# Sliding-window caches loaded once for all four groups, unchanged cache rows copied HBM to HBM, first group's sample rows two tiles later

## The chip, the core and the metric

The kernel runs on one core of one Trainium2 chip. The metric is the device time of one execution in microseconds, as the median of several runs; lower is better.

## What is computed

One inference step of a hybrid decoder layer, in float32, for 1024 prompt tokens and 8 sample tokens (one new token for each of 8 requests). From the normalised tokens `h` one wide projection gives the inputs of two branches, retention (4 heads) and sliding-window attention (16 query heads in 4 groups, one key and value head of 64 for each group); both are gated, projected, merged by sigmoid gates and projected once more. The change concerns the sample tokens of the sliding-window branch:

```python
def swa_sample(q, k, v, sinks, cache_k, cache_v):
    kk = jnp.concatenate([cache_k.astype(k.dtype), k], axis=1)
    vv = jnp.concatenate([cache_v.astype(v.dtype), v], axis=1)
    ...
    o = sink_attention(q[:, None], kk[:, None], vv[:, None], allowed, sinks)[:, 0]
    return o, kk[:, Ts:], vv[:, Ts:]
```

The caches are (8 requests, 128 rows, 4 groups, 64). Each request attends to the last 127 cached rows and its new row. The outputs `ks` and `vs` are the caches moved up by one row, with the new row at the end: 127 of 128 rows of each are copies of the input.

## The kernel before

All matrix products run on TensorE as three products of a split into an upper and a lower half (`hi`, `lo`). A weight unit is loaded into `wraw` on SP's queue (`load_unit`, L162), ACT makes the upper half `whi` (L168), and POOL the lower half `wlo` (L169). There are three `wraw` buffers and six of each half, and `run_steps` loads units ahead of their use.

`groups` builds one long list of steps: first the loading and normalising of the tokens (`norm_h`), then eight groups, four of retention (`ret_tile`, `ret_rows`) and four of sliding window (`swa_tile`, `swa_rows`). A group goes over eight tiles of 128 tokens. In each tile a product of 128 tokens with 384 columns (`gemm_tok`, L222 to L224) is followed by the tile's other stages, which are spread over the next tiles as a pipeline, and between them stand fill blocks: gates of the group before (`gate_block`, products L212 to L214, then tanh on ACT, a product on DVE and, on POOL, L288) and merge gates (`mg_block`, whose results leave on ACT's own DMA queue, L299). `FILL`, `TAIL` and `ROW` say how many fill blocks a group gets, how many come after its last tile, and after which tile the 8 sample rows of a group start. The rows run as stages as well, one after each following tile.

`swa_rows` of a group g takes these steps: load the 127 last rows of the group's keys into `cK` and of its values into `cV` (L569, L570; partition = cache row, so a DMA writes 127 partitions of 8 rows of 64 floats, 256 B each); project the 8 sample rows (`gemm_rows`, L232, L233, and L237 into `rkv`), rope and norm (`kd`); put the new key and value into partition 127 (L575, L576); store the whole of `cK` and `cV` to the outputs (L577, L578); then, one stage each, transpose queries (L585) and keys (L592), scores (L599), softmax, product with the values (L612). `cK` and `cV` have one buffer each.

`swa_consts` runs once, when the sliding-window groups begin: it loads rope tables, band, sinks (L848, eight small DMAs).

The order on each engine and queue is not the order of the code: a scheduler puts the instructions of all steps in an order by its own times, and each engine then takes them strictly in that order. An instruction that waits holds all that stand behind it on its engine. Every DMA of SP goes to one queue that is served by up to 16 DMA engines; a DMA of SP also waits for the DMA eight places ahead of it that used its semaphore.

Of the kernel before, what the change touches and what calls it, by code (L numbers as in the profile page):

```python
# [17 lines left out]
P = 128  # L18
D = 1024
SEQ = 1024  # L20
NS = 8
# [6 lines left out]
SH, KVH, G, HD = 16, 4, 4, 64  # L28
# [25 lines left out]
QAT = (1, 2, 4)  # L54
ROW = [2, 0, 0, 0, 0, 0, 0, 1]
FILL = [3, 2, 2, 2, 9, 9, 9, 4]
# [66 lines left out]
class Body:  # L123
# [25 lines left out]

# [1 line left out]
    def load_unit(self, spec):  # L151
# [46 lines left out]

# [1 line left out]
    def mm3(self, ps, a, b, start=True, stop=True):  # L200
# [37 lines left out]

# [1 line left out]
    def norm_h(self, t):  # L240
# [36 lines left out]

# [1 line left out]
    def gate_block(self, unit, kt, nb, oT, i):  # L279
# [20 lines left out]

# [1 line left out]
    def ret_q(self, unit, qT, nb):  # L302
# [145 lines left out]

# [1 line left out]
    def rope_s(self, dst, src, A, B, nh, t, p=P):  # L450
# [114 lines left out]
    def swa_rows(self, g, units, oT):  # L565
        nc = self.nc
        K = self.t(self.ap, [P, NS, HD], "cK", bufs=1)
        V = self.t(self.ap, [P, NS, HD], "cV", bufs=1)
        nc.sync.dma_start(out=K[: P - 1], in_=self.i["cache_swa_k"][0, :, 1:, g, :].rearrange("b k d -> k b d"))  # L569
        nc.sync.dma_start(out=V[: P - 1], in_=self.i["cache_swa_v"][0, :, 1:, g, :].rearrange("b k d -> k b d"))  # L570
        acc = self.t(self.pacc, [P, 512], "acc")
        kv = self.t(self.ap, [NS, 384], "rkv", bufs=1)
        self.gemm_rows(acc[:MROW, :384], units, self.hs, kv[:], 384)
        qr, kd, rs = self.swa_rope(kv[:], NT, NS)
        nc.sync.dma_start(out=K[P - 1 : P], in_=kd[:NS, 0, :])  # L575
        nc.sync.dma_start(out=V[P - 1 : P], in_=kv[:, 320:384])  # L576
        nc.sync.dma_start(out=self.o["ks"][0, :, :, g, :].rearrange("b k d -> k b d"), in_=K[:])  # L577
        nc.sync.dma_start(out=self.o["vs"][0, :, :, g, :].rearrange("b k d -> k b d"), in_=V[:])  # L578
        qn = self.t(self.ap, [NS, G, 2, HD], "rbig", bufs=1)
# [9 lines left out]
        pt = self.t(self.ptr, [P, 512], "tr")  # L589
        kc = K[:].rearrange("p b d -> p (b d)")  # L590
        for i in range(NS // 2):
# [4 lines left out]
        R = NS * G  # L596
# [11 lines left out]
        pTs = self.t(self.ap, [P, R], "pTs", bufs=1)  # L608
        nc.scalar.activation(out=pTs[:], in_=pt[:, :R], func=AF.Copy)
        yield  # L610
        po = self.t(self.pav, [P, 512], "av")
        nc.tensor.matmul(po[:R], pTs[:], V[:].rearrange("p b d -> p (b d)"), start=True, stop=True)  # L612
        od = self.t(self.ap, [R, NS, HD], "rbig", bufs=1)
# [32 lines left out]

# [1 line left out]
    def build(self):  # L648
# [38 lines left out]
    def groups(self):  # L687
        nc = self.nc
# [16 lines left out]
        def gates(gi, st):  # L705
            for i in range(2):
                kt = 2 * gi + i
                col = (OFF_RG + kt * P) if gi < 4 else (OFF_SG + (kt - 8) * P)
                for nb in range(NB):
                    yield ([tch(col)], (lambda us, kt=kt, nb=nb, i=i: self.gate_block(us[0], kt, nb, st["o"], i)))  # L710
# [10 lines left out]
        kv = slabs([(OFF_RK, DK), (OFF_RV, DV)])  # L721
# [12 lines left out]
        def rope_block(nb):  # L734
# [3 lines left out]
            return ([], fn, 0)  # L738

        def tables(us):  # L740
            nc.sync.dma_start(out=self.ropeK[:], in_=self.i["c_ropeK"][:])
            nc.sync.dma_start(out=self.misc[:], in_=self.i["c_misc"][:])
            nc.sync.dma_start(out=self.maskT[:], in_=self.i["c_maskT"][:])
# [12 lines left out]
        for gi in range(8):  # L756
# [5 lines left out]
            if ret:  # L762
# [10 lines left out]
                kv = slabs([(OFF_RK + h * DK, DK), (OFF_RV + h * DV, DV)])  # L773
                mk = lambda u, t, h=h, st=st: self.ret_tile(h, t, u, st["q"], st, st["o"])
                mkr = lambda u, h=h, st=st: self.ret_rows(h, u, st["q"], st["o"])
            else:
                g = gi - 4
# [7 lines left out]
                kv = slabs([(OFF_SQ + g * G * HD, G * HD), (OFF_SK + g * HD, HD), (OFF_SV + g * HD, HD)])  # L785
# [30 lines left out]
            if extra:  # L816
                pipe = []
            prev = list(gates(gi, st))

# [15 lines left out]
    def swa_consts(self):  # L835
        nc, ap = self.nc, self.ap
        self.swa_tables()
        nc.sync.dma_start(out=self.rng[:], in_=self.i["ret_norm_g"][0].rearrange("h (i p) -> p (h i)", p=P))
        nc.vector.tensor_scalar(out=self.rng[:], in0=self.rng[:], scalar1=0.5, scalar2=None, op0=ALU.mult)
        self.band = self.t(ap, [P, 2 * P], "band")  # L840
        nc.sync.dma_start(out=self.band[:], in_=self.i["c_band"][:])
        self.sink = self.t(ap, [P, SH], "sink")
        nc.sync.dma_start(out=self.sink[:], in_=self.i["swa_sinks"][0:1, :].broadcast_to([P, SH]))
        self.nsink = self.t(ap, [P, SH], "nsink")
        nc.vector.tensor_scalar(out=self.nsink[:], in0=self.sink[:], scalar1=-1.0, scalar2=None, op0=ALU.mult)
        self.sinkr = self.t(ap, [NS * G, KVH], "sinkr")
        for b in range(NS):
            nc.sync.dma_start(out=self.sinkr[b * G : (b + 1) * G, :], in_=self.i["swa_sinks"][0].rearrange("(g j) -> j g", g=KVH))  # L848
        self.nsinkr = self.t(ap, [NS * G, KVH], "nsinkr")
        nc.vector.tensor_scalar(out=self.nsinkr[:], in0=self.sinkr[:], scalar1=-1.0, scalar2=None, op0=ALU.mult)  # L850

    def split_op(self, pool, tag, src, kt):
# [121 lines left out]
```

## Time and profile before

| | |
|---|---|
| time, median of 3 runs | 1224.25 us (1223.89 to 1225.06) |
| span of the profiled execution | 1217.8 us |
| between that span and the median | 6.45 us |
| TensorE busy | 1178.2 us, 97% of the span |
| VectorE, ScalarE, GpSimd busy | 679.5, 457.9, 353.5 us |
| mean granted TensorE clock | 0.993 of full speed |
| moved by DMA | 116.69 MB, mean 96 GB/s |
| largest wait of TensorE | 17.7 us |

The page gives, for one execution, the busy time of each engine, the span in 40 slices of 30.4 us with the busy share in tenths, and the groups of instructions that cost most. The trace can be asked for more: who waited for whom, the instructions of one engine in order of time, and for any stretch the busy time, the granted clock (1.00 is 2.4 GHz, 0.50 is 1.2 GHz), the busy share of the 16 DMA engines (transfers that overlap on an engine count twice, so it can pass 1) and the GB/s. SPq stands for SP's DMA queue, and the time of a row there is the time that issuing took, not the transfer.

### The profile page before, as it was taken

Reading aid. Unit: us, or ns where it says so; the run is one execution under the profiler, and the core shown is the slowest. Engines: PE = TensorE matmul, PEld = TensorE weight load, DVE = VectorE, ACT = ScalarE, POOL = GpSimd, SP = SyncE. Lnnn points to the kernel's source line nnn. Section 1 sums busy time; section 2 is a strip of 40 time slices with the busy share of each in tenths; the row PEclk is TensorE's granted clock in tenths of the full one; section 3 lists DMA queues with packets and bytes.
Section 4 is the critical chain, followed back from the end, with each engine's and each line's share of the span. In section 5 each row is a group of like instructions: output and inputs, shape, how many; then the busy total and the mean of one; then the engine's idle time right before and its main releaser. Section 6 shows DMA issues by size and latency. Waiting matters only on the chain.

```text
span 1217.8 us, 19525 instructions
## 1 busy us (share of the span) xinstructions
PE 1178.2 (97%) x7228; PEld 1112.4 (91%) x7228; DVE 679.5 (56%) x2018; ACT 457.9 (38%) x1158; POOL 353.5 (29%) x278
## 2 busy tenths in 40 slices
PE   5999999999999859999999999999999999999998
PEld 5899999999999759999999999999899999999876
DVE  5854554544554438787677688578854411565121
ACT  6544342443343124554454445444544310221010
POOL 5434035116126312331342125222523122122010
PEclk9999999999999979999999999999999999999999
DMA  9133204214114112230142014201516844554221
GB/s 321 49 94 102 68 22 123 75 42 122 59 37 121 58 32 63 79 105 20 36 132 82 16 36 125 72 24 36 170 41 230 249 143 144 170 162 136 79 88 69
DMA packets 139368, 116.69 MB, mean 96 GB/s; under 512 B 33760, under 2 KB 127456, under 8 KB 139272
## 3 DMA queue, kind: packets, MB, share of 16 engines
q1 hardware_dynamic: 132360, 106.98, 29.0%
q10 hardware_dynamic: 6912, 8.46, 2.0%
q8 instruction: 57, 0.93, 0.3%
q14 instruction: 39, 0.32, 0.1%
HBM read 82.95 MB, written 32.44 MB: 95 GB/s over the span
## 4 chain that ended last, share of the span: by engine, by line
PE 89%; DVE 4%; DMA 2%; SPq 1%; ACT 1%; issue 1%; POOL 1%; ACTq 0%; POOLq 0%
PE acc L212 15%; PE acc L213 15%; PE acc L214 15%; PE acc L224 9%; PE acc L223 9%; PE acc L222 9%; PE tr L546 2%; DVE s L491 1%; DMA cV<-rkv 1%; PE acc L233 1%; PE acc L232 1%; PE av L441 1%; PE sc L532 1%; PE sc L533 1%; SPq L570 1%; PE av L557 1%
## 5 line engine op out<-in xcount | busy, mean ns | idle before, releaser
L169 POOL TENSOR_TENSOR wlo<-wraw,whi 128x1024 fp32r<-128x1024 f32 (+1 forms) x92 | 205.2, 2240 | 333.7 <-ACT whi L168 276.4
L212 PE MATMUL acc<-hhi,whi 128*128 128x344 f32 x864 | 281.2, 326 | 0.6 <-ACT tg L298 0.6
L213 PE MATMUL acc<-hlo,whi 128*128 128x344 f32 x864 | 278.4, 322 | 0.0
L214 PE MATMUL acc<-hhi,wlo 128*128 128x344 f32 x864 | 278.3, 323 | 0.0
L222 PE MATMUL acc<-whi,hhi 128*128 128x384 f32 x512 | 174.7, 342 | 1.7 <-ACT hhi L139 1.3
L224 PE MATMUL acc<-whi,hlo 128*128 128x384 f32 x512 | 174.9, 342 | 0.0
L223 PE MATMUL acc<-wlo,hhi 128*128 128x384 f32 x512 | 174.3, 340 | 0.6 <-POOL wlo L169 0.6
L212 PEld LDWEIGHTS acc<-hhi,whi 128*128 128x128 f32 x864 | 163.1, 189 | 2.8 <-ACT tg L298 0.9
L213 PEld LDWEIGHTS acc<-hlo,whi 128*128 128x128 f32 x864 | 162.9, 188 | 1.9 <-issue 1.0
L214 PEld LDWEIGHTS acc<-hhi,wlo 128*128 128x128 f32 x864 | 162.7, 188 | 1.1 <-issue 0.4
L147 POOL TENSOR_TENSOR rs<-ms,nhalf 128x1 f32<-128x1 f32 (+3 forms) x81 | 69.4, 859 | 322.4 <-DVE ms L146 318.1
L168 ACT ACTIVATE whi<-wraw 128x1024 fp32r<-128x1024 f32 (+1 forms) x92 | 90.1, 982 | 156.2 <-PE acc L213 97.9
L222 PEld LDWEIGHTS acc<-whi,hhi 128*128 128x128 f32 x512 | 96.6, 189 | 3.1 <-ACT hhi L139 1.7
L223 PEld LDWEIGHTS acc<-wlo,hhi 128*128 128x128 f32 x512 | 96.6, 189 | 2.4 <-POOL wlo L169 1.0
L224 PEld LDWEIGHTS acc<-whi,hlo 128*128 128x128 f32 x512 | 96.5, 188 | 0.8 <-DVE hlo L140 0.2
L486 ACT ACTIVATE s<-s,ng 128x256 f32<-128x256 f32 (+1 forms) x128 | 61.7, 485 | 27.0 <-DVE ng L483 26.6
L288 POOL TENSOR_TENSOR oT<-oT,tg 128x344 f32<-128x344 f32 x48 | 45.7, 954 | 88.3 <-DVE tg L286 60.7
L536 DVE CUSTOM_DVE_ANT_0 s<-sc,band,rs 128x256 f32<-128x256 f32 (+1 forms) x128 | 53.6, 459 | 13.1 <-PE sc L533 12.8
L139 ACT ACTIVATE pThi<-tr 128x512 fp32r<-128x512 f32 x60 | 35.3, 597 | 52.3 <-PE tr L546 51.8
L140 DVE TENSOR_TENSOR pTlo<-tr,pThi 128x512 fp32r<-128x512 f32 x60 | 40.9, 685 | 23.0 <-ACT pThi L139 22.6
L491 DVE TENSOR_SCALAR s<-s,r 128x256 f32<-128x256 f32 (+1 forms) x128 | 52.9, 475 | 0.7
L224 PE MATMUL acc<-whi,mlo 128*128 128x512 f32 x128 | 50.5, 395 | 0.0
(345 smaller groups left out, 2365.1 us busy)
## 6 DMA issues: line engine op xcount, KB each, us to landing
wraw<-in_w_in SPq DMA_DIRECT2D x36, 512.0 KB
d_t<-tg ACTq DMA_DIRECT2D x48, 172.0 KB
d_o<-oT SPq DMA_DIRECT2D x16, 516.0 KB
tt<-d_t SPq DMA_DIRECT2D x48, 172.0 KB
wraw<-in_w_in SPq DMA_DIRECT2D x32, 256.0 KB
st<-d_o SPq DMA_DIRECT2D x9, 516.0 KB
d_m<-tt SPq DMA_DIRECT2D x24, 172.0 KB
mm<-d_m SPq DMA_DIRECT2D x24, 172.0 KB
```

Of the source, the lines that this page charges most:

```text
L147: nc.gpsimd.tensor_tensor(out=rs[:p, :width], in0=ms[:p, :width], in1=self.nhalf[:p, :width], op=ALU.pow)
L168: nc.scalar.activation(out=hi[:, :f], in_=raw[:, :f], func=AF.Copy)
L169: nc.gpsimd.tensor_tensor(out=lo[:, :f], in0=raw[:, :f], in1=hi[:, :f].bitcast(F32), op=ALU.subtract)
L212: nc.tensor.matmul(ps, whi[:, k, :], hi[:, cs], start=(k == 0), stop=False)
L213: nc.tensor.matmul(ps, whi[:, k, :], lo[:, cs], start=False, stop=False)
L214: nc.tensor.matmul(ps, wlo[:, k, :], hi[:, cs], start=False, stop=(k == KT - 1))
L222: nc.tensor.matmul(ps, hi[:, k, a:b], whi[:, kk, :], start=(k == 0), stop=False)
L223: nc.tensor.matmul(ps, hi[:, k, a:b], wlo[:, kk, :], start=False, stop=False)
L224: nc.tensor.matmul(ps, lo[:, k, a:b], whi[:, kk, :], start=False, stop=(k == KT - 1))
L486: nc.scalar.activation(out=s[:p, j, :nk], in_=s[:p, j, :nk], func=AF.Exp, bias=ng[:p, j : j + 1], accum_out=l[:p, j : j + 1])
L491: nc.vector.tensor_scalar(out=s[:p, j, :nk], in0=s[:p, j, :nk], scalar1=r[:p, j : j + 1], scalar2=None, op0=ALU.mult)
L536: nc.vector.tensor_tensor_reduce(out=s[:, j, :nk], in0=sc[:, a, :nk], in1=band, scale=rs[:, j : j + 1], scalar=-3e38, op0=ALU.add, op1=ALU ...
```

## The change

The loads of `cK` and `cV` leave `swa_rows`. Two tiles of (128, 8, 256) are kept for all four groups, and `swa_consts` loads each of them once, in rows of 1 KB (all four groups of one cache row of one request). `swa_rows` works on the 64 columns of its group, and POOL first copies the group's keys into a dense tile `kc` for the transposes. Only the new row is stored from SBUF; the 127 unchanged rows are copied from the input to the output in HBM, by `shift`, a step put behind group 1's tiles. Group 4 of the list (the first sliding-window group) has its rows two tiles later (`ROW`).

```diff
-ROW = [2, 0, 0, 0, 0, 0, 0, 1]
+ROW = [2, 0, 0, 0, 2, 0, 0, 1]
...
     def swa_rows(self, g, units, oT):
         nc = self.nc
-        K = self.t(self.ap, [P, NS, HD], "cK", bufs=1)
-        V = self.t(self.ap, [P, NS, HD], "cV", bufs=1)
-        nc.sync.dma_start(out=K[: P - 1], in_=self.i["cache_swa_k"][0, :, 1:, g, :].rearrange("b k d -> k b d"))
-        nc.sync.dma_start(out=V[: P - 1], in_=self.i["cache_swa_v"][0, :, 1:, g, :].rearrange("b k d -> k b d"))
+        gs = slice(g * HD, (g + 1) * HD)
+        K, V = self.cK[:, :, gs], self.cV[:, :, gs]
...
         nc.sync.dma_start(out=K[P - 1 : P], in_=kd[:NS, 0, :])
         nc.sync.dma_start(out=V[P - 1 : P], in_=kv[:, 320:384])
-        nc.sync.dma_start(out=self.o["ks"][0, :, :, g, :].rearrange("b k d -> k b d"), in_=K[:])
-        nc.sync.dma_start(out=self.o["vs"][0, :, :, g, :].rearrange("b k d -> k b d"), in_=V[:])
+        nc.sync.dma_start(out=self.o["ks"][0, :, P - 1, g, :], in_=kd[:NS, 0, :])
+        nc.sync.dma_start(out=self.o["vs"][0, :, P - 1, g, :], in_=kv[:, 320:384])
...
-        kc = K[:].rearrange("p b d -> p (b d)")
+        kc = self.t(self.ap, [P, NS, HD], "kc", bufs=1)
+        nc.gpsimd.tensor_copy(out=kc[:], in_=K)
+        kc = kc[:].rearrange("p b d -> p (b d)")
...
-        nc.tensor.matmul(po[:R], pTs[:], V[:].rearrange("p b d -> p (b d)"), start=True, stop=True)
+        nc.tensor.matmul(po[:R], pTs[:], V, start=True, stop=True)
...
+        def shift(us):
+            for o, name in (("ks", "cache_swa_k"), ("vs", "cache_swa_v")):
+                nc.sync.dma_start(
+                    out=self.o[o][0, :, : P - 1].rearrange("b k g d -> b (k g d)"),
+                    in_=self.i[name][0, :, 1:].rearrange("b k g d -> b (k g d)"),
+                )
...
+            if gi == 1:
+                put(([], shift))
...
     def swa_consts(self):
         nc, ap = self.nc, self.ap
+        self.cK = self.t(ap, [P, NS, KVH * HD], "cK")
+        self.cV = self.t(ap, [P, NS, KVH * HD], "cV")
...
+        for dst, name in ((self.cK, "cache_swa_k"), (self.cV, "cache_swa_v")):
+            nc.sync.dma_start(out=dst[: P - 1], in_=self.i[name][0, :, 1:].rearrange("b k g d -> k b (g d)"))
...
-    nc = bacc.Bacc("TRN2", target_bir_lowering=False, num_devices=1)
+    nc = bacc.Bacc("TRN2", target_bir_lowering=False, num_devices=1, dynamic_dma_scratch_size=1024)
```

The scheduler moves more than the diff tells. First, SP's queue near the start of the program, as a difference of the two orders (the line numbers are those of each kernel; `ropeT`, `rng` and `oT` are tables, norm weights and tiles of x, `wraw_270` holds the query weights of the first group):

```order
 L737 DMA ropeT_140<-in_c_ropeT 128x2x344
-L838 DMA rng_111<-in_ret_norm_g 128x8x1
+L742 DMA out_ks<-in_cache_swa_k 8x2x16256
+L742 DMA out_vs<-in_cache_swa_v 8x2x16256
 L162 DMA wraw_270<-in_w_in 128x8x128
+L849 DMA rng_111<-in_ret_norm_g 128x8x1
 L251 DMA oT_299<-in_x_prompt 128x1024 x2
 L162 DMA wraw_398<-in_w_in 128x8x128
```

The copies of `shift`, written behind group 1, stand ahead of the query weights and of the last tiles of x; the load of `rng` has gone behind those weights.

Second, SP's queue where the sliding-window groups begin, before and then after (`sinkr` are the small tables, `wraw_6055` the first weights of the second sliding-window group):

```order
L848 DMA sinkr_4809<-in_swa_sinks 4x4x1 x8
L569 DMA cK_4899<-in_cache_swa_k 127x8x64
L570 DMA cV_4900<-in_cache_swa_v 127x8x64
L576 DMA cV_4900<-rkv_4904 1x8x64
L578 DMA out_vs<-cV_4900 128x8x64
L575 DMA cK_4899<-kd_4944 1x8x64
L577 DMA out_ks<-cK_4899 128x8x64
L569 DMA cK_6359<-in_cache_swa_k 127x8x64
L162 DMA wraw_6055<-in_w_in 128x2x256
```

```order
L859 DMA sinkr_4813<-in_swa_sinks 4x4x1 x8
L863 DMA cK_4780<-in_cache_swa_k 127x8x256
L863 DMA cV_4781<-in_cache_swa_v 127x8x256
L574 DMA cV_4781<-rkv_5137 1x8x64
L576 DMA out_vs<-rkv_5137 8x64
L573 DMA cK_4780<-kd_5177 1x8x64
L575 DMA out_ks<-kd_5177 8x64
L162 DMA wraw_6055<-in_w_in 128x2x256
```

The two loads keep their place and their 127 partitions, and their rows grow from 64 to 256 floats; the new rows still follow them on the queue.

Third, POOL in the first sliding-window group, before and then after (`oT<-oT,tg` is a gate's product, `rs` a tile's rstd, `wlo_5341` before and `wlo_5309` after the lower half of the next gate block's weights):

```order
L147 TENSOR_TENSOR rs_5180<-ms_5179,nhalf_68 128x5
L288 TENSOR_TENSOR oT_3572<-oT_3572,tg_5298 128x344
L169 TENSOR_TENSOR wlo_5341<-wraw_5339,whi_5340 128x1024
L288 TENSOR_TENSOR oT_3572<-oT_3572,tg_5334 128x344
L147 TENSOR_TENSOR rs_5375<-ms_5374,nhalf_68 128x5
```

```order
L288 TENSOR_TENSOR oT_3574<-oT_3574,tg_5266 128x344
L589 COPY kc_5371<-cK_4780 128x512
L169 TENSOR_TENSOR wlo_5309<-wraw_5307,whi_5308 128x1024
L288 TENSOR_TENSOR oT_3574<-oT_3574,tg_5302 128x344
L147 TENSOR_TENSOR rs_5343<-ms_5342,nhalf_68 128x5
```

The copy of the keys stands directly ahead of that lower half. On PE the same gate block now has this beginning, behind the last products of a tile, and the transposes of the keys come only after it:

```order
L224 MATMUL acc_5313<-whi_4836,hlo_122 128x384
L212 MATMUL acc_5441<-hhi_121,whi_5308 128x344
L213 MATMUL acc_5441<-hlo_122,whi_5308 128x344
L214 MATMUL acc_5441<-hhi_121,wlo_5309 128x344
L212 MATMUL acc_5441<-hhi_121,whi_5308 128x344
```

Before, the transposes stood earlier, in the middle of the gate block ahead of that one:

```order
L214 MATMUL acc_5273<-hhi_121,wlo_4845 128x344
L592 MATMUL tr_5040<-ident_63,cK_4899 128x128 x4
L212 MATMUL acc_5273<-hhi_121,whi_4844 128x344
L512 MATMUL tr_5049<-ident_63,qr_4882 128x128 x2
L513 MATMUL tr_5049<-ident_63,kd_4894 128x128
```

So what PE meets first is no longer the transpose of the keys but the third product of the gate block.

## Rows read from the trace of the kernel before

**Rows 1.** The page: span, busy time of the engines, PE in 40 slices.
```profile
span 1217.8 us, 19525 instructions
...
PE 1178.2 (97%) x7228; PEld 1112.4 (91%) x7228; DVE 679.5 (56%) x2018; ACT 457.9 (38%) x1158; POOL 353.5 (29%) x278
...
PE   5999999999999859999999999999999999999998
```

**Rows 2.** Waits of PE: waited for, us in total, times, longest.
```profile
PE tr L592 <- DMA cK<-kd: 17.7, 1, 17.7
PE tr L271 <- DVE oT L266: 7.9, 1, 7.9
PE tr L271 <- DVE hlo L140: 4.5, 4, 2.2
```

**Rows 3.** Windows: busy us of each engine, granted clock, DMA share, GB/s.
```profile
core 0: us, PE busy (x) PEld busy (x) DVE busy (x) ACT busy (x) POOL busy (x), PEclk, DMA share, GB/s
424.00:437.00 13.00, 0.00 (x0) 0.00 (x0) 0.00 (x0) 0.00 (x0) 0.00 (x0) 0.63 0.08 18
428.00:441.00 13.00, 0.12 (x1) 0.15 (x2) 0.14 (x1) 0.00 (x0) 0.00 (x0) 0.50 0.14 34
441.00:445.00 4.00, 4.00 (x18) 3.96 (x19) 3.18 (x14) 1.58 (x4) 1.17 (x1) 0.57 0.28 68
445.00:456.00 11.00, 11.00 (x74) 10.54 (x73) 7.23 (x26) 4.81 (x16) 4.23 (x3) 1.00 0.08 19
560.00:820.00 260.00, 259.43 (x1630) 246.15 (x1630) 190.10 (x678) 126.05 (x361) 75.28 (x52) 1.00 0.21 62
```

**Rows 4.** Timeline of SP's queue, 406 to 441: start, us of issuing.
```profile
406.91 0.26 SPq L569 DMA_DIRECT2D cK<-in_cache_swa_k  x1
407.21 14.27 SPq L570 DMA_DIRECT2D cV<-in_cache_swa_v  x1
421.58 14.36 SPq L576 DMA_DIRECT2D cV<-rkv  x1
438.00 0.42 SPq L578 DMA_DIRECT2D out_vs<-cV  x1
438.52 0.69 SPq L575 DMA_DIRECT2D cK<-kd  x1
```

**Rows 5.** Windows in a state load's stream and in one of 4 KB rows.
```profile
43.70:44.70 1.00, 0.00 (x0) 0.00 (x0) 0.95 (x3) 0.92 (x2) 0.33 (x1) 1.00 1.05 373
15.00:16.00 1.00, 1.00 (x8) 1.00 (x8) 0.68 (x1) 0.80 (x2) 1.00 (x2) 1.00 1.02 418
```

**Rows 6.** Timeline of PE: row matmul, key transposes, the gate block before.
```profile
395.46 0.33 PE L232 MATMUL acc<-whi,hs 128*40 128x384 f32 x1
...
440.88 0.45 PE L592 MATMUL tr<-ident,cK 128*128 128x128 f32 x1 [17.70 <-DMA cK<-kd]
...
456.07 0.32 PE L212 MATMUL acc<-hhi,whi 128*128 128x344 f32 x1
```

**Rows 7.** Groups of POOL by form: count, busy us, mean ns, idle before.
```profile
L169 POOL TENSOR_TENSOR wlo<-wraw,whi 128x1024 fp32r<-128x1024 f32 x60 | 144.1, 2406 | 291.8 <-ACT whi L168 234.5 <-PE acc L233 42.8 <-DMA d_t<-tg 8.9
L288 POOL TENSOR_TENSOR oT<-oT,tg 128x344 f32<-128x344 f32 x48 | 45.7, 954 | 88.3 <-DVE tg L286 60.7 <-DVE oT L563 10.1 <-DVE l L488 7.5
```

**Rows 8.** Near the start: a window, then SP's queue, DVE, ACT and PE.
```profile
2.00:32.00 30.00, 19.35 (x107) 17.40 (x108) 19.21 (x36) 19.19 (x35) 15.90 (x12) 1.00 1.05 339
...
16.68 2.43 SPq L162 DMA_DIRECT2D wraw<-in_w_in  x1
...
23.74 1.78 DVE L839 TENSOR_SCALAR rng<-rng 128x8 f32<-128x8 f32 x1
...
24.25 1.06 ACT L168 ACTIVATE whi<-wraw 128x1024 fp32r<-128x1024 f32 x1
...
29.03 0.32 PE L212 MATMUL acc<-hhi,whi 128*128 128x344 f32 x1
```

## Prediction

> **What bounds the kernel now.** I read the page's busy shares first: PE works for 1178.2 of 1217.8 us, with a weight load beside almost every matmul, and in the 40 slices it is at 9 tenths nearly everywhere [rows 1]. So only what makes PE wait, or keeps it from waiting, can move the time. The list of PE's waits names one wait that matters after the first 8 us: 17.70 us for the DMA `cK<-kd` [rows 2]. The windows show its place. From 424 to 437 us no engine does anything, while the DMA engines are 0.08 busy and move 18 GB/s [rows 3]; the granted clock goes to 0.50 meanwhile and is at 1.00 again from 445, so about 4 us of work after the wait run at half speed, some 2 us more. The DMA queue of SP says why [rows 4]: the two cache loads of the first sliding-window group are issued from 406.91, the second issue is held for 14.27 us and the one behind it for 14.36 us, and only at 438.52 can `cK<-kd` go, which the transposes at 440.88 need [rows 6]. That wait is all the change can win, 17.7 + 2 = 19.7 us. Groups 1 to 3 load their caches the same way, but PE has no wait on them; taking those loads away is worth nothing on PE.
>
> The rate matters most. One cache load is 127 x 8 rows of 256 B, 260,096 B. In 14.3 us that is 18.2 GB/s, and the all-idle window has the same 18 GB/s at a DMA share of 0.08, about one engine of 16 [rows 3, 4]. A load over 128 partitions is another thing: the state load, also in 1 KB rows, moves 373 GB/s, and a stretch of 4 KB rows 418 GB/s [rows 5]. Per engine that is 23.3 and 26.1 GB/s. So a cache load runs on one engine, near that engine's own pace. I read this as a matter of its 127 partitions: nothing else in its form differs from a transfer that fills all 16.
>
> The Trainium skill has this as a rule (DMA: Bandwidth & Descriptors, "Why a DMA increments its semaphore by 16 and not by 1"): the number of engines is the largest up to 16 that divides the slowest dimension, and 127 partitions get one. The trace agrees (18 GB/s). By the same page's specifications an engine moves about 27 GiB/s, an estimate of 72 us for the two new loads, and the sum below would be about 1264.
>
> **The change, part by part.**
>
> *Loads of 1 KB rows.* The new loads take all four groups: 127 x 8 x 1 KB, 1,040,384 B each, again with 127 partitions outermost, so again one engine. At 23.3 GB/s (the row with the same row size) one takes 44.6 us and both 89.3. The ends: 79.7 us at 26.1 GB/s, 114.2 at the 18.2 GB/s of the present loads. They stand behind the same small table loads in SP's order, so the first is issued at about 406.9 again. Before, 33.9 us pass from that issue to the landing of `cK<-kd` (it is followed by PE at 440.88), of which 28.63 are the two streams; 5.3 are the rest, and about 2 of these fall away because the store of the new value row no longer waits for a copy into cV. So `cK<-kd`, which is issued behind both loads and shares their first engine, lands at 406.9 + 89.3 + 3.8 = 500.0.
>
> *Rows two tiles later.* The sample rows of group 0 are now projected after the third tile, not the first. The transposes of the keys no longer stand in front of PE, which is the gain meant. But the order on POOL shows a new wait: the copy `kc<-cK` needs both cK transfers, and directly behind it in POOL's order stands the lower half `wlo_5309` of a gate's weights, which PE wants three matmuls into the next gate block. Behind that come a gate's product and a tile's rstd; DVE and PE wait for those too. When does PE get there? From 395.46 (the first row matmul) to 456.07 (the same gate block before) are 60.6 us [rows 6]; less 17.7 of wait and 2.1 of half clock, less some 2.2 for transposes and scores of the rows that now come after it, that is 38.6 us of work: PE arrives at 434.0. The copy has no row; by columns of a POOL product of 344 (0.954 us [rows 7]) 512 columns are 1.4, by a plain one-input copy less; I take 1.2 (0.6 to 1.5). The lower half is 2.41 us [rows 7]. So PE goes on at 500.0 + 1.2 + 2.4 = 503.6: **a stall of 69.6 us where 17.7 stood**, net 51.9. The clock's fall and return cost about the same 2 us once either way. SP too is blocked by the long streams until about 495, but its next issues are the weights of group 1, wanted some 60 us of PE work later; the merge-gate stores go out on ACT's own queue.
>
> *Groups 1 to 3.* Eight loads and eight 256 KB stores become eight stores of 2 KB, and three `kc` copies join POOL, which works 75.3 of the 260 us from 560 to 820 [rows 3]: nothing on the path.
>
> *Unchanged rows HBM to HBM.* The scheduler puts these two copies at the front, ahead of the query weights. They go out as 8 rows of two 65,024 B pieces; as 128 rows fill 16 engines and 127 one, I take 8 rows to go to 8 engines. Both copies then put 260,096 B on each of the 8: 10.0 us at 26.1 GB/s, 14.3 at 18.2. From 2 to 32 us the DMA engines are full (1.05, 339 GB/s) [rows 8], so all that is queued behind is later by as much. First wanted are the query weights: issued 16.68 to 19.11, taken up by ACT at 24.25, used by PE at 29.03 [rows 8]. ACT came straight from other work, so they had landed some time before 24.25; I take 23. Plus 10.0, plus 1.06 for the upper half, PE starts at 34.1, 5 us late. The tiles of x behind have that slack again. Ends: the multiply by `rng`, which held DVE for 1.78 us there [rows 8], is moved back, so a copy that costs nothing would gain 1.8; landing at 24.25 and 14.3 us make it 10.6 late.
>
> **Sum**: 1224.25 - 17.7 + 69.6 + 5 = **1281 us**. The page's span is 1217.8, 6.45 under the median of the runs; the sum is made of differences, so I set it on the median and take the surroundings of the span as unchanged.
>
> **Rivals.**
>
> *The loads spread over 16 engines (faster).* At 373 GB/s both take 5.6 us, all has landed by 415, `cK<-kd` by about 430 (the row projection ends some 12 us before PE's 434, and the DMA takes 2.4 us from 438.52 to 440.88), and the copy and the lower half are ready near 434 when PE comes: no stall. 1224.25 - 19.7 + 5 = 1209.5, or 1203 if the front copy also costs nothing. It decides as soon as the two streams are through by 430, at 2.08 MB in 21 us, 100 GB/s or over four engines. For it: the bytes per partition row are four times larger. Against: the 18 GB/s of rows 3 belong to a transfer with the same outer dimension. Chance 6%. [...]
>
> *A row costs the same whatever its size (about the same).* 1016 rows in 14.3 us are 14 ns a row; were that a price per row, the loads would still take 28.6 us together, PE would go on at 442.9, a stall of 8.9, and the sum is 1220. Against: 1 KB rows at 23.3 GB/s are 44 ns each. Chance 2%, of no difference as of a small gain.
>
> *The front copy is the larger or the smaller loss (slower).* Hidden wholly: 1274. At 10.6: 1287. Together with the ends of the streams these are the forecast's own spread.
>
> **How the numbers follow.** Forecast 91%, spread case 6%, per-row case 2%, something else 1%. Within the forecast: streams -9.6 to +24.9, front copy -6.8 to +5.6, the arrival and the copy's rows 2 either way. All low ends at once give 1263, all high ones 1313; the high end of the streams is the pace of 256 B rows, farther off than the low one, so I end the range at 1303. Range 1263 to 1303. About 0.2%, 2.4 us, is what can be told from no change here. Slower by over that: 92%; faster: 6.5%; within: 1.5%.
>
> **What would show it.** Right: SP's issue of cV held for some 40 us and the one behind it again; a window after 440 with all engines idle and about 23 GB/s; PE's largest wait at the gate block behind `wlo`, POOL's at `kc<-cK` for a DMA, 60 us or more; granted clock 0.50 within; a wait of about 5 us near 30 us. Wrong: the loads land within 20 us of their issue, or PE passes 434 to 500 without a gap (forecast fallen); the stream is 80 or 114 us (size off); no wait near 30 us (the front copy is hidden).

## The result and the profile after

| | before | after |
|---|---|---|
| time, median of 4 runs each | 1224.28 us (1223.89 to 1225.06) | 1277.24 us (1276.74 to 1278.05) |
| span of the profiled execution | 1217.8 us | 1276.3 us |
| mean granted TensorE clock | 0.993 | 0.971 |

The ratio is 1.0436, with a 95% interval of 1.0421 to 1.0452: the change costs 53 us. It was forecast at 1281, within 1263 to 1303.

The page after, with the lines that answer to [rows 1], and the row of granted clock:

```profile
span 1276.3 us, 19496 instructions
...
PE 1184.9 (93%) x7228; PEld 1118.0 (88%) x7228; DVE 667.8 (52%) x2018; ACT 457.5 (36%) x1158; POOL 354.6 (28%) x282
...
PE   5899999999999900999999999999999999999998
...
PEclk9899999999999955999999999999999999999999
```

PE has as many matmuls as before and is busy only 6.7 us longer, while the span grew by 58.5. So most of the loss is idle time, and the slices say where: two of 31.9 us each, numbers 15 and 16, have next to no PE work, at about half the clock.

PE's waits after (what waited, for what: us in total, times, longest), which answer to [rows 2]:

```profile
PE acc L214 <- POOL wlo L169: 60.9, 1, 60.9
PE tr L271 <- DVE oT L266: 7.9, 1, 7.9
PE acc L212 <- ACT whi L168: 6.5, 1, 6.5
```

The 17.7 us for `cK<-kd` are gone from PE's list. Two large waits are new: 60.9 us for a lower half on POOL, and 6.5 us for an upper half on ACT. Neither POOL nor ACT is the cause. POOL's timeline (start, us, what, and in brackets the idle time ahead with its releaser) shows what held it:

```profile
438.40 0.92 POOL L288 TENSOR_TENSOR oT<-oT,tg 128x344 f32<-128x344 f32 x1
504.39 0.61 POOL L589 COPY kc<-cK 128x512 f32<-128x512 f32 x1 [65.07 <-DMA cK<-kd]
504.96 2.34 POOL L169 TENSOR_TENSOR wlo<-wraw,whi 128x1024 fp32r<-128x1024 f32 x1
```

PE's timeline shows the other side of the same wait:

```profile
446.12 0.31 PE L213 MATMUL acc<-hlo,whi 128*128 128x344 f32 x1
507.36 0.66 PE L214 MATMUL acc<-hhi,wlo 128*128 128x344 f32 x1 [60.92 <-POOL wlo L169]
507.81 0.49 PE L212 MATMUL acc<-hhi,whi 128*128 128x344 f32 x1
```

PE had its upper half and did two products with it. The third wants `wlo`, which stands behind `kc<-cK` on POOL, and that copy waits for the new key row. Why the key row is late stands on SP's queue, to be laid beside [rows 4] (a row's time is that of issuing, not of the transfer):

```profile
412.54 0.26 SPq L863 DMA_DIRECT2D cK<-in_cache_swa_k  x1
424.37 29.50 SPq L863 DMA_DIRECT2D cV<-in_cache_swa_v  x1
453.96 44.07 SPq L574 DMA_DIRECT2D cV<-rkv  x1
498.08 0.46 SPq L576 DMA_DIRECT2D out_vs<-rkv  x1
498.64 0.67 SPq L573 DMA_DIRECT2D cK<-kd  x1
```

The issues behind the two loads are held for 29.50 and 44.07 us where 14.27 and 14.36 stood. In 44.07 us one load of 1,040,384 B goes by: 23.6 GB/s. Windows (length, busy us of PE, PEld, DVE, ACT and POOL with their counts, granted clock, DMA share, GB/s), of the stream, of the restart and of a place much later:

```profile
440.00:495.00 55.00, 6.43 (x41) 6.15 (x39) 7.33 (x41) 5.75 (x22) 0.00 (x0) 0.60 0.07 24
507.30:512.60 5.30, 5.24 (x18) 5.25 (x19) 0.00 (x0) 0.00 (x0) 2.00 (x3) 0.50 0.52 174
925.00:929.00 4.00, 4.00 (x18) 3.97 (x18) 3.89 (x15) 2.44 (x5) 0.95 (x1) 0.61 1.11 341
```

All engines are idle for most of 55 us while the DMA engines are 0.07 busy, about one engine of 16, and move 24 GB/s. The granted clock falls to 0.50 in the wait and stays there for 5.2 us of work behind it. There is one more stretch at half clock near 925 us, of 3.4 us, that the profile of before does not have. It is not the change's own: PE waits 1.79 us for `s` just ahead of it, at 924.76, as it does for 1.80 us at 869.06 in before with no fall of the clock behind it; and e6 below, the kernel before with other loads and stores, has both the wait (1.80 us at 850.97) and the fall (0.81 from 849 to 858).

Now the start, first before and then after, the same three windows:

```profile
24.00:30.00 6.00, 3.83 (x25) 3.65 (x26) 5.06 (x12) 4.38 (x8) 3.82 (x2) 1.00 1.08 342
30.00:38.00 8.00, 8.00 (x52) 7.96 (x52) 7.77 (x18) 6.52 (x13) 7.57 (x5) 1.00 0.33 86
38.00:60.00 22.00, 19.93 (x133) 18.55 (x131) 16.60 (x47) 10.06 (x30) 4.99 (x8) 1.00 0.14 43
```

```profile
24.00:30.00 6.00, 3.01 (x18) 2.51 (x18) 4.97 (x18) 2.78 (x7) 1.35 (x1) 1.00 0.46 177
30.00:38.00 8.00, 4.04 (x13) 4.04 (x14) 1.42 (x3) 3.71 (x6) 3.76 (x3) 0.60 0.93 287
38.00:60.00 22.00, 18.17 (x110) 16.43 (x109) 11.93 (x28) 8.92 (x20) 9.10 (x9) 0.91 0.33 89
```

From 24 to 60 us PE is busy 31.76 us before and 25.22 after: 6.5 us more idle. And it runs slower: from 30 to 38 the 4.04 us of work are at half clock (2.0 us lost), and from 38 to 60 the mean is 0.91 of full speed (0.09 x 22, at most another 2.0, since PE is not at work in all of it). That makes some 10 us. How late everything is afterwards can be read off SP, at a place ahead of the cache loads, before and then after:

```profile
395.42 0.36 SPq L391 DMA_DIRECT2D out_rp<-S  x1
```

```profile
406.04 0.36 SPq L391 DMA_DIRECT2D out_rp<-S  x1
```

10.6 us, so the three windows hold nearly all of it. ACT's timeline names the transfer that was late, the query weights, behind the two copies HBM to HBM on the queue:

```profile
32.85 1.06 ACT L168 ACTIVATE whi<-wraw 128x1024 fp32r<-128x1024 f32 x1 [3.46 <-DMA wraw<-in_w_in]
```

A profile is one execution, though, and the clock part of such a loss comes and goes without the change. e1 below is the program of before but for a scratch size; PE has the same 2.2 us wait near 26 us in both profiles, and only e1's goes to half clock behind it:

```profile
24.00:30.00 6.00, 3.81 (x16) 3.81 (x17) 3.71 (x6) 3.56 (x6) 3.83 (x2) 0.72 1.08 342
```

Over all profiles SP's row `out_rp<-S` stands at 395.1 to 398.5 us in the seven kernels without a copy at the front, and at 404.3 to 407.5 in the four that have it as in the change. The means are 9.5 us apart.

### The profile page after: what moved, and what is told of

Read it like the earlier page. It is cut to its first block, busy times and chain, and to the rows that moved or that the text cites. A ratio compares the mean times of both kernels' runs of the same rounds, so it can differ in the third digit from the quotient of the medians.

```text
span 1276.3 us, 19496 instructions
## 1 busy us (share of the span) xinstructions
PE 1184.9 (93%) x7228; PEld 1118.0 (88%) x7228; DVE 667.8 (52%) x2018; ACT 457.5 (36%) x1158; POOL 354.6 (28%) x282
## 4 chain that ended last, share of the span: by engine, by line
PE 85%; SPq 6%; DVE 3%; DMA 3%; ACT 1%; issue 1%; POOL 1%; ACTq 0%; POOLq 0%
PE acc L212 14%; PE acc L214 14%; PE acc L213 14%; PE acc L224 9%; PE acc L223 9%; PE acc L222 9%; SPq L574 3%; SPq L863 2%; PE tr L546 2%; PE av L441 1%; DMA oT<-in_x_prompt 1%; PE acc L232 1%; PE acc L233 1%; PE av L557 1%; PE sc L532 1%; DVE s L491 1%
## 5 line engine op out<-in xcount | busy, mean ns | idle before, releaser
L214 PE MATMUL acc<-hhi,wlo 128*128 128x344 f32 x864 | 280.3, 325 | 60.9 <-POOL wlo L169 60.9
```

What stands on the lines that cost most here:

```text
L214: nc.tensor.matmul(ps, wlo[:, k, :], hi[:, cs], start=False, stop=(k == KT - 1))
```

## The experiments

Theory: the change loses at two separate places. The cache loads run on one DMA engine, because they write 127 partitions, and hold up the key row; and the copies HBM to HBM delay the first weights by their place at the front. Rivals: the loads are slow for another reason (their row size, or any count under 128), the stall comes from the new place of the sample rows, or the front copy is hidden. Times are compared by their ratio to runs of the kernel before on the same chip, which ran at medians of 1222.08 to 1223.68 us there; a ratio times 1224.28 gives the figure "on the first chip" in the table at the end.

**e1_scratch.** The kernel before with the one line of the change that I had left out of the sum.

```diff
-    nc = bacc.Bacc("TRN2", target_bir_lowering=False, num_devices=1)
+    nc = bacc.Bacc("TRN2", target_bir_lowering=False, num_devices=1, dynamic_dma_scratch_size=1024)
```

> The kernel before with the smaller DMA scratch size as its only edit. Between the profiled executions the span grew by 58.5 us (1217.8 to 1276.3), the median only by 53.0; 5.5 us went somewhere outside the span. Theory: the scratch size takes them from what lies around the span, so 1224.3 - 5 = 1219, with a span near 1217.8. Rival: it does nothing, the 5.5 us are the profiled execution's own; then 1224.3.

1222.63 us, ratio 0.9996 (0.9982 to 1.0009): nothing. The theory in it fell. What it did show is the time around the span: its profiled execution took 1222.14 us with a span of 1220.3, so 1.8 us, as for the changed kernel (1278.05 and 1276.3). So the 6.45 us between the span of before and its median [rows 1] are mostly the difference between one execution and a median: with 1.8 us around its span, that execution took some 1219.6 (an estimate from these two rows). The 17 runs of the kernel before on that chip scatter from 1220.4 to 1226.75 us, the fastest with a mean granted clock of 0.993 and the slowest with 0.987.

**e2_noshift.** The change without the copies HBM to HBM; it leaves the 127 unchanged rows of both outputs unwritten.

```diff
-            if gi == 1:
-                put(([], shift))
```

> The changed kernel without the copy of the unchanged cache rows from HBM to HBM: rows 0 to 126 of the two sample cache outputs are not written. Theory: that copy at the front, on 8 engines, costs all of the 10.6 us by which PE reaches the row products later (a wait of 6.5 for the query weights, the rest at half clock); the wait in the first sliding-window group stays near 61 us, since its end hangs on when the cache loads are issued. So 1277.2 - 10.6 = 1266.6, between 1264 and 1270. Rival as the prediction had it: 5 us, 1272. Rival that the copy is hidden: 1277.

1266.23 us, ratio 1.0350 (1.0333 to 1.0367), 10.5 us under the change by the ratios. PE's waits, for the query weights no longer and for POOL as ever:

```profile
PE acc L214 <- POOL wlo L169: 60.6, 1, 60.6
PE tr L271 <- DVE oT L266: 8.2, 1, 8.2
PE tr L271 <- DVE hlo L140: 4.5, 4, 2.2
```

The first cache load goes out 9.4 us sooner than in the change, and PE comes to it sooner as well, so the wait is the same:

```profile
403.16 0.26 SPq L861 DMA_DIRECT2D cK<-in_cache_swa_k  x1
```

The two losses are separate and add.

**e3_spread.** The change with its loads over all 128 partitions. Row 0 of the cache, which nothing needs, is loaded too, and the new row takes its place in partition 0.

```diff
-            nc.sync.dma_start(out=dst[: P - 1], in_=self.i[name][0, :, 1:].rearrange("b k g d -> k b (g d)"))
+            nc.sync.dma_start(out=dst[:], in_=self.i[name][0].rearrange("b k g d -> k b (g d)"))
...
-        nc.sync.dma_start(out=K[P - 1 : P], in_=kd[:NS, 0, :])
-        nc.sync.dma_start(out=V[P - 1 : P], in_=kv[:, 320:384])
+        nc.sync.dma_start(out=K[0:1], in_=kd[:NS, 0, :])
+        nc.sync.dma_start(out=V[0:1], in_=kv[:, 320:384])
```

> The changed kernel with the two cache loads over 128 partitions instead of 127: row 0 is loaded too, into partition 0, and the new row overwrites partition 0. The bytes grow by 1/127. Theory: only the 127 partitions keep the loads on one engine; with 128 both take about 6 us, the wait of 60.9 us and the 2.6 us lost to half clock behind it go, so 1277.2 - 63.5 = 1214, with PE waiting nowhere over 3 us after 40 us. Rival: it is the bytes or the strided rows of 1 KB themselves that are slow; then the wait stays and the time is over 1260.

1213.80 us, ratio 0.9918 (0.9902 to 0.9934). One more partition of 128 takes 63 us off. SP's queue, and a window in the stream:

```profile
413.90 0.40 SPq L863 DMA_DIRECT2D cK<-in_cache_swa_k  x1
422.71 0.40 SPq L863 DMA_DIRECT2D cV<-in_cache_swa_v  x1
434.79 0.73 SPq L574 DMA_DIRECT2D cV<-rkv  x1
```

```profile
416.00:418.00 2.00, 2.00 (x15) 1.98 (x14) 0.82 (x2) 0.00 (x0) 0.00 (x0) 1.00 1.02 340
```

No issue is held, the engines are full at 340 GB/s, and PE has no wait over 1.2 us in the group; of the two losses only the 6.5 us at the start are left.

**e7_two.** Is it one engine because 127 is under 128, or because 127 has no divisor? The same 127 rows in two pieces.

```diff
-            nc.sync.dma_start(out=dst[: P - 1], in_=self.i[name][0, :, 1:].rearrange("b k g d -> k b (g d)"))
+            for k0, k1 in ((0, 122), (122, P - 1)):
+                nc.sync.dma_start(out=dst[k0:k1], in_=self.i[name][0, :, 1 + k0 : 1 + k1].rearrange("b k g d -> k b (g d)"))
```

> The changed kernel with each cache load cut in two transfers, of 122 and of 5 partitions; bytes, row size and order as they were. Theory (the number of engines is the largest up to 16 that divides the outermost dimension: 2 for 122, 5 for 5): the long piece has 999,424 B on two engines, 21.5 us each at 23.3 GB/s an engine, the two loads together some 43 to 46 us in place of 88; PE's wait behind wlo falls from 60.9 to 16 to 20 us, 1277.2 - 43 = 1234 (1231 to 1238). Rival (anything under 128 partitions goes to one engine): no change, 1277. Rival (each transfer is cut into 16 whatever it is, and 127 was slow for another reason): 1214 to 1218.

1231.62 us, ratio 1.0072 (1.0053 to 1.0091). SP's queue, and a window in the stream:

```profile
410.69 18.15 SPq L864 DMA_DIRECT2D cK<-in_cache_swa_k  x2
428.88 21.43 SPq L864 DMA_DIRECT2D cV<-in_cache_swa_v  x2
450.41 0.74 SPq L574 DMA_DIRECT2D cV<-rkv  x1
```

```profile
432.00:448.00 16.00, 12.65 (x82) 12.37 (x81) 12.81 (x60) 7.07 (x27) 2.05 (x2) 1.00 0.14 48
```

Twice the rate, 48 GB/s at a share of 0.14, about two engines; PE's wait behind `wlo` is 15.6 us. Both rivals fell: 122 partitions are neither as slow as 127 nor as fast as 128.

**e6_spread256.** The kernel before, with its rows of 256 B and its order, and only the partitions of the loads changed as in e3 (and the stores of the unchanged rows cut into 112 and 15 partitions).

```diff
-        nc.sync.dma_start(out=K[: P - 1], in_=self.i["cache_swa_k"][0, :, 1:, g, :].rearrange("b k d -> k b d"))
+        nc.sync.dma_start(out=K[:], in_=self.i["cache_swa_k"][0, :, :, g, :].rearrange("b k d -> k b d"))
...
+        for o, c in (("ks", K), ("vs", V)):
+            for k0, k1 in ((1, 113), (113, P)):
+                nc.sync.dma_start(out=self.o[o][0, :, k0 - 1 : k1 - 1, g, :].rearrange("b k d -> k b d"), in_=c[k0:k1])
...
```

> The kernel before, its rows of 256 B, its order and ROW as they were; only the loads go over 128 partitions (row 0 is loaded too, and the new row goes to partition 0), and the stores leave in pieces of 112 and 15 partitions. Theory (the 17.7 us wait of PE came from 127 partitions on one engine, not from the size of the rows or from where the rows stand): each load is through in some 2 to 3 us, PE passes the key transposes without a wait, and the 17.7 and some 2 of half clock go: 1224.3 - 19.7 = 1204.6 (1203 to 1208). Rival (256 B rows are slow by themselves, on any number of engines): the wait stays at 10 us or more, 1216 to 1224.

1205.09 us, ratio 0.9855 (0.9839 to 0.9871). PE's wait for `cK<-kd` is gone with neither larger rows nor later ones. A window in its two loads:

```profile
409.50:411.50 2.00, 2.00 (x15) 2.00 (x14) 1.68 (x2) 0.25 (x1) 2.00 (x4) 1.00 1.07 234
```

Rows of 256 B on full engines move 234 GB/s, against 18 on one [rows 3]. What row size adds beyond that (340 in e3) no PE wait here depends on.

**e4_row2 and e10_row0.** The one line on the sample rows, alone in the kernel before, and undone in the change.

```diff
-ROW = [2, 0, 0, 0, 0, 0, 0, 1]
+ROW = [2, 0, 0, 0, 2, 0, 0, 1]
```

> The kernel before with the first sliding-window group's sample rows two tiles later as its only edit; loads of 256 B rows for each group as before. Theory: the loads still take 28.6 us on one engine, but PE meets the key transposes only near 442, after the landing of the new row near 441; the wait of 17.7 us and the 2 us at half clock go, 1224.3 - 19.7 = 1204.6. Rival: the wait moves along, onto POOL or DVE or a later product, 1215 to 1224.

1204.20 us, ratio 0.9839 (0.9825 to 0.9853). The loads are as slow as before, and `cK<-kd` is issued at nearly the same time as in [rows 4], but PE now comes to the transposes only at 446.75 and finds it done:

```profile
436.64 0.69 SPq L575 DMA_DIRECT2D cK<-kd  x1
```

```profile
446.75 0.27 PE L592 MATMUL tr<-ident,cK 128*128 128x128 f32 x1
```

> The changed kernel with ROW[4] back at 0: the sample rows of the first sliding-window group start after the first tile again, all else as in the change. Theory (the stream ends at the same time whatever stands behind it, so the order only sets what PE gets done before it must wait): cK<-kd lands near 504 as in the changed kernel, PE comes to the key transposes at 423.2 + 10.6 = 433.8 and waits for kc there till about 505, some 71 us in place of 60.9, 1277.2 + 10 = 1287 (1283 to 1290). Rival (the new place of the rows is what makes the stall, since it put the copy ahead of a gate's lower half): the rows at their old place wait less than 60.9 us, 1277 or less.

1289.12 us, ratio 1.0531 (1.0500 to 1.0561), 12 us over the change by the ratios:

```profile
PE tr L592 <- POOL kc L589: 74.0, 1, 74.0
```

So the later rows are the good part of the change. Alone they win 19.7 us, as [rows 2, 3] priced the wait (17.7 + 2); in the change they shorten the stall from 74.0 to 60.9 us. The rival, that their place makes the stall, fell. A part of this is on SP's queue, where the eight small table loads ahead of the cache loads take 8.65 us with the rows at their old place and 3.66 with the later ones (before, e10 and the change; what holds them was not traced):

```profile
398.21 8.65 SPq L848 DMA_DIRECT2D sinkr<-in_swa_sinks  x8
410.11 8.65 SPq L859 DMA_DIRECT2D sinkr<-in_swa_sinks  x8
408.83 3.66 SPq L859 DMA_DIRECT2D sinkr<-in_swa_sinks  x8
```

**e8_front16 and e9_late.** What is it about the front copies: that they run on eight engines, or that they stand ahead of the weights? Both start from e3_spread. e8 writes each copy as 16 outer slices of 8 pieces of 8,128 B.

```diff
-                    out=self.o[o][0, :, : P - 1].rearrange("b k g d -> b (k g d)"),
-                    in_=self.i[name][0, :, 1:].rearrange("b k g d -> b (k g d)"),
+                    out=self.o[o][0, :, : P - 1].rearrange("b k g d -> b (k g d)").rearrange("b (s x) -> s b x", s=16),
+                    in_=self.i[name][0, :, 1:].rearrange("b k g d -> b (k g d)").rearrange("b (s x) -> s b x", s=16),
```

> The kernel with spread loads (1213.8), with the front copy HBM to HBM written as 16 outer slices of 8 pieces of 8,128 B in place of 8 rows of two 65,024 B. Theory (the 10.6 us come from eight engines that each carry 260,096 B ahead of the query weights): over 16 engines the copy holds them half as long, PE's start is late by some 5 us less, 1208 to 1210. Rival (the front is full of bytes in any case, 1.05 busy at 339 GB/s from 2 to 32 us, so all of the 2.08 MB, read and written, delays the weights however it is spread): 1212 to 1214, the same as with 8 rows.

1212.25 us, ratio 0.9910 (0.9893 to 0.9927), 1 us under e3 and not to be told from it. In the trace PE's wait for the query weights did fall, from 6.5 to 3.1 us. The three windows of e8, and behind them the last two of e3:

```profile
24.00:30.00 6.00, 3.01 (x18) 2.51 (x18) 5.03 (x19) 3.29 (x8) 1.29 (x1) 1.00 1.04 287
30.00:38.00 8.00, 7.46 (x36) 7.44 (x37) 1.70 (x5) 6.07 (x11) 7.18 (x5) 0.79 1.02 311
38.00:60.00 22.00, 17.73 (x100) 16.14 (x99) 11.90 (x27) 6.46 (x17) 5.68 (x7) 0.84 0.15 44
```

```profile
30.00:38.00 8.00, 4.06 (x15) 4.07 (x16) 1.44 (x3) 3.46 (x6) 3.64 (x3) 0.57 0.89 287
38.00:60.00 22.00, 17.65 (x103) 16.14 (x102) 11.88 (x28) 9.17 (x20) 9.07 (x9) 0.87 0.34 90
```

The DMA share from 24 to 30 is 1.04, where the change with its 8 rows has 0.46. PE has 3.4 us more of work from 30 to 38 than in e3 and about as much from 38 to 60, at nearly the same clock there; SP's row `out_rp<-S` stands at 404.14 in place of 407.51. So between these two profiles the 3.4 us are kept, while the medians show 1 us, with an interval of some 3 us either way. The theory's 1208 to 1210 was missed by the median. What spreading the copy is worth, from nothing to those 3.4 us, stays open.

e9 leaves the copies as they are and puts them behind the cache loads:

```diff
...
+        for o, name, src in (("ks", "cache_swa_k", self.cK), ("vs", "cache_swa_v", self.cV)):
+            nc.sync.dma_start(out=self.o[o][0, :, 0].rearrange("(o b) g d -> o b (g d)", o=1), in_=src[1:2])
+            nc.sync.dma_start(
+                out=self.o[o][0, :, : P - 1].rearrange("b k g d -> b (k g d)"),
+                in_=self.i[name][0, :, 1:].rearrange("b k g d -> b (k g d)"),
+            )
```

> The kernel with spread loads (1213.8), its two copies HBM to HBM as they are (8 rows of two 65,024 B, on eight engines) but issued behind the cache loads: a store of the first kept row out of the loaded tile, which the copy then writes over, goes ahead of each and ties the copy to that place. Theory (the copy's 10.6 us are a price of its place at the front, ahead of the query weights and the tiles of x, and near 410 us the DMA engines have room): PE starts the query product near 29 us, no wait of PE over 3 us in the first sliding-window group, 1203 to 1206. Rival (the copy also costs behind the loads, since the new value and key rows and the next weights queue behind 260,096 B on each of eight engines, some 10 us): a new wait of PE of 4 us or more behind cK<-kd or a wlo there, 1208 or more.

1205.69 us, ratio 0.9851 (0.9824 to 0.9878), some 8 us under e3. The same copies in the same form cost nothing that shows there: the next row on SP's queue is not held, and POOL waits 2 us for the key row.

```profile
416.88 0.74 SPq L857 DMA_DIRECT2D out_ks<-in_cache_swa_k  x1
418.08 0.69 SPq L857 DMA_DIRECT2D out_vs<-in_cache_swa_v  x1
422.44 0.71 SPq L574 DMA_DIRECT2D cV<-rkv  x1
```

So it is their place that costs; whether their form adds to it at the front, e8 leaves open.

**e5_best.** The change with both losses taken out the other way: spread loads as in e3, no copy HBM to HBM as in e2, and the unchanged rows stored from SBUF behind the loads.

```diff
...
+        for src, o in ((self.cK, "ks"), (self.cV, "vs")):
+            for k0, k1 in ((1, 113), (113, P)):
+                nc.sync.dma_start(out=self.o[o][0, :, k0 - 1 : k1 - 1].rearrange("b k g d -> k b (g d)"), in_=src[k0:k1])
```

> The changed kernel with three edits: cache loads over all 128 partitions (the new row goes to partition 0), no copy HBM to HBM, and the 127 unchanged rows stored from SBUF in two pieces of 112 and 15 partitions straight behind the loads. Theory (the two losses of the change, the one-engine stream and the front copy, are separate and add): 1213.8 (the kernel with spread loads) less the 10.6 of the front copy, 1203; PE starts the query product near 29 us again and has no wait over 3 us in the first sliding-window group. Rival (the 2 MB of stores behind the loads fill the queues, and the sample rows or the next weights come late): a new wait of PE of 5 us or more behind cK<-kd or a wlo, 1208 or more.

1204.68 us, ratio 0.9853 (0.9836 to 0.9870): the theory's 1203 within the interval, no new wait.

| kernel | ratio to before | on the first chip | PE's waits that differ |
|---|---|---|---|
| before | 1 | 1224.3 | 17.7 |
| the change | 1.0436 | 1277.2 | 60.9 + 6.5 |
| change, rows at their old place (e10) | 1.0531 | 1289.3 | 74.0 + 6.5 |
| change, no front copy (e2) | 1.0350 | 1267.1 | 60.6 |
| change, loads in 122 + 5 (e7) | 1.0072 | 1233.1 | 15.6 + 6.3 |
| change, loads spread (e3) | 0.9918 | 1214.2 | 6.5 |
| e3, front copy on 16 engines (e8) | 0.9910 | 1213.3 | 3.1 |
| e3, copy behind the loads (e9) | 0.9851 | 1206.0 | none |
| e3, stores from SBUF (e5) | 0.9853 | 1206.3 | none |
| before, loads spread (e6) | 0.9855 | 1206.5 | none |
| before, rows two tiles later (e4) | 0.9839 | 1204.6 | none |

The last four can't be told from each other, and all beat both kernels. The one with the smallest edit is e4: one number, without any of the rest of the change. Together the repairs can win no more than that, since the only wait to win was the 17.7 us and its clock.

## Why the prediction was right, step by step

The sum was 1281 and the time 1277.24; two terms were off by 6 to 9 us in opposite directions, so that it came this close is in part luck.

| term of the sum | predicted | measured, by spans |
|---|---|---|
| the wait that goes | -17.7 | -17.7 |
| the stall in its place | +69.6 | +60.9 |
| the front copies | +5 | +10.6 |
| the clock behind the stall | 0 | +0.9 (5.2 us at half clock, 3.4 before: 2.6 - 1.7) |
| the clock near 925 us | not seen | +1.7 (3.4 us at half clock) |
| two short waits of PE (1.0 for `opA7h` at 1005.01, 0.7 for `s` at 640.99) | not seen | +1.7 |
| not traced | | +0.4 |
| sum | +56.9 | +58.5 |

- **Loads of 1 KB rows: right.** One engine, 23.3 GB/s and 89.3 us for both were forecast; 23.6 GB/s in SP's held issue came, and from the first load's issue at 412.54 to POOL's copy at 504.39 went 91.9 us, where 406.9 to 500.0, 93.1, were forecast. The inference from 127 partitions, made from two rows of before, was the heart of it, and e3 and e7 show it: 1, 2 and 16 engines for 127, 122 and 128 partitions. The step said that nothing else in the slow load's form differs, but its rows were of 256 B beside 1 KB and 4 KB; e6 shows that this was not the cause. The rule of the Trainium skill (DMA: Bandwidth & Descriptors, "Why a DMA increments its semaphore by 16 and not by 1"), the largest divisor up to 16 of the outermost dimension, gives 1, 2 and 16, and these traces agree. By the pace of one engine on the same page of the Trainium skill, 72 us would be the estimate for both loads; the measurement decides for the row's 23.3 GB/s.
- **Rows two tiles later: the mechanism right, the stall 8.7 us too long.** PE was to come to the gate block at 434.0 and go on at 503.6. It came at 446.43 and went on at 507.36. The place, the waiting copy and `wlo` behind it are as forecast. The 10.6 us of the start move both ends of the stall, the loads and PE, as the 60.6 us of e2 show. Without them PE came 1.8 us later than forecast, work and short idle stretches that the step sized too small, and went on 6.9 us sooner. Of these, 5.0 are the first load: the step took the table loads ahead of it as unchanged, and they took SP 3.66 us where 8.65 had stood. The way from the load to the copy was 1.3 shorter (0.5 of it a slip: 5.3 less 2 is 3.3 and not 3.8), and the copy took 0.61 us, under the 1.2 assumed (0.6 to 1.5). The lower half took 2.34, as forecast.
- **Unchanged rows HBM to HBM: the step that failed in size, 10.6 for 5.** The wait itself was right: PE took up the query product at 33.96 where 34.1 was forecast. What the step left out comes behind it: 1.6 us more idle time among the late tiles of x, which the prediction thought had "that slack again", and two stretches at half clock, up to 4.0 us together. It priced the fall of the clock for the long stall and forgot it for the short one. How much of the clock's part is the copies' own varies: the 10.6 stand against a profile of before that has no such stretch, the mean over the profiles is 9.5, and by the medians the copies cost 10.5 us (the change against e2) and 8 (e3 against e9). The upper end of 10.6 held by chance, as it was worked out from other terms. e9 shows that their form, 8 rows of two 65,024 B pieces, is no loss by itself behind the loads.
- **Groups 1 to 3: right.** POOL's `kc` copy is waited for by nobody there: of 71.3 us that the four copies waited, 65.1 are the first one's, and no wait of PE over 3 us stands in those groups.
- **The sum's footing: wrong, small.** The surroundings of the span were taken as 6.45 us. They are 1.8 (e1), so the sum stood on a median that lies 4.7 us above the execution that its durations came from. That is why the spans differ by 58.5 and the medians by 53.0.
- **The rivals.** Loads spread over 16 engines: it did not go so, but its price was good, as e3 made the case true: 1214.2 where 1209.5 was worked out, 4.7 more, by about the term of the front copy. A price per row fell with the 44.07 us.

## What to carry to other kernels

Before a transfer is made larger, work out from an existing one of the same outer shape how many engines carry it: held issues on the queue, and a window with a DMA share near 1/16, say one, and then more bytes per row only make the one stream longer. Change the outer dimension (load a row too many, and put the new one in its place), or give the consumer more slack, which alone was enough here. A copy that nothing waits for still costs if a scheduler puts it ahead of the first weights; tie it to a later place. A lateness ahead of a stall moves both of its ends where the transfer is late with it, so it adds to the time in full; and a short wait can cost clock as a long one does.

## What was not expected of the hardware

- A PE wait of 6.5 us at the start was followed by half clock (0.54 from 31 to 38 us), and waits of under 2 us each around 47 to 55 by another such stretch (0.57 from 55 to 59): up to 4 us lost on top of the wait. e1, with the instructions of before, has one as well (0.72 from 24 to 30) behind a wait of 2.2 us that before passes at full clock, so which wait brings one is not shown.
- A stream on one DMA engine held SP itself, not only the transfers behind it: 73.6 us in two issues, with 15 other engines free.
- Executions of the kernel before differ by 0.5% among themselves (1220.4 to 1226.75 over 17 on one chip), wider than the 1.2 us of the first four runs, and the mean granted clock goes from 0.993 to 0.987 with them, so a span of one profile can lie 5 us from a median.
